# Attention's product with V in two matmuls instead of three: both parts of V as one weight tile, and row differences of V instead of differences of the running products

## The chip, the cores and the metric

The kernel is one launch on one core of a Trainium2 chip. The metric is the device time of an execution in microseconds. Before the change it is 1157.95, the median of three timed executions (1156.58, 1157.95 and 1157.99). Times below are microseconds unless marked otherwise.

## What is computed

The reference is a trunk of two layers on a sequence of 512 tokens of width 1024. Layer 0 mixes the tokens with a stick-breaking attention of 16 heads of 64 columns, layer 1 with a gated token-mixing block; each mixer is followed by a SwiGLU block. All of them stand between RMS norms and a modulation by a conditioning vector. Only the attention bears on this change:

```python
def stick_breaking_attention(q, k, v):
    scale = SB_HEAD_DIM ** -0.5
    for qb in range(S // SB_QBLOCK):
        q0 = qb * SB_QBLOCK
        kend = q0 + SB_QBLOCK
        z = jnp.einsum('bhtd,bhsd->bhts', q[:, :, q0:kend], k[:, :, :kend]) * scale
        before = s_idx < t_idx
        log_beta = jax.nn.log_sigmoid(z)
        log_1m = jnp.where(before, jax.nn.log_sigmoid(-z), 0.0)
        later = lax.cumsum(log_1m, axis=3, reverse=True) - log_1m
        a = jnp.where(before, jnp.exp(log_beta + later), 0.0)
        outs.append(jnp.einsum('bhts,bhsd->bhtd', a, v[:, :, :kend]))
```

A query's weight for an earlier token s is sigmoid(z_s) times the product of sigmoid(-z) over the tokens between s and the query. If r_s is the running product of sigmoid(-z), counted from the query backwards, the weight is the difference of two neighbouring running products. The sum over s of (r before s - r after s) v_s can be regrouped by the running products: each r then multiplies the difference of two neighbouring rows of V.

## The kernel before, in words

The sequence is handed over in reverse order of time, so that "later" runs to the right and one scan along the free dimension forms the running products. Every operand of a matmul is held as two parts, a rounded high part and the rest as a low part, each in a 32-bit matmul type. A product is the sum of three matmuls, high by high, high by low and low by high (`mm3`, L104 to L107). `split` (L112 to L117) makes the two parts: ACT copies the source into the high part, DVE subtracts that from the source.

**Weights** come by DMA from SP's queue into `raw` tiles (two buffers), are split into `wh` (ACT, L159) and `wl` (DVE, L160), and are asked for by `wget` (up to L238) three tiles ahead of use. The columns of the modulation (`G`, `A`, `B` tiles) are summed on DVE out of `rawada` tiles by a background generator; one call of `ada_step` does one step of it.

**The order of instructions.** From the attention stage on PE runs in the order in which the program is written (`pe["chain"]`, set ahead of the second half of V), and DVE from the end of the second half of V until the end of the stage (`dve.chain`). ACT throughout, and DVE ahead of that point, run in the order that the framework's scheduler picks. An engine runs its instructions in that fixed order: one that waits holds up those behind it.

**V.** The projection of V is computed in two halves of 512 columns (8 heads each). `v_step` (L616) adds one of eight contraction steps to four PSUM banks, one for each tile of 128 tokens. `v_evac` (L621) splits the four banks into `Vh` and `Vl` in SBUF (slots at L613 and L614). The first half is done under the start of the layer and evacuated at L739. The second half runs from 64.8 to 90.6 in the trace; between its steps stand the scores of the first pair of heads, and it is evacuated at L933.

**Attention** works on pairs of heads, eight of them, in a loop at the end of the stage (up to L975). Inside a pair (`attend`, L822):

- `scores` (L839) is called for key blocks 3 and 1 together (`B31`), 2 (`B2`) and 0 (`B0`). PE makes z of both heads with three matmuls for each block and head, into two banks `zb`. ACT writes the sigmoid of -z into a tile `ga` (L861). DVE runs one scan along the free dimension, which multiplies the running product by each element (`left`, one tile, shifted by one column), and then subtracts the shifted `left` from `left` back into `ga`: these are the attention weights. There are four `ga` tiles in rotation. Masks `ones` (made with `gaps`) restart the product at the block edges.
- `flip` (L874) turns 128x128 blocks of weights with PE transposes into a bank `tw`, and splits that into `ar` (two buffers): ACT the high part, DVE the low part. It is called for three groups of blocks: `LATE`, `EARLY[0]` and `EARLY[1]`.
- `values` (L888) multiplies with V. For each token block, the V columns of both heads of the pair (128 columns) are the stationary weights, and `ar` of one head is streamed; each of the two heads has its own bank `av` of 128 rows, of which only the 64 rows of that head are used. `mm3` makes it three matmuls.
- `finish` (L903): ACT copies the 64 rows of each head out of `av` into one tile `of` (L909), which is split into `o`, the input of the output projection.

The loop of one pair reads: flip `LATE`, fill, scores `B31` of the next pair, fill, values `LATE`, fill, flip `EARLY[0]`, fill, scores `B2` of the next pair, fill, values `EARLY[0]`, flip `EARLY[1]`, fill, scores `B0` of the next pair, fill, values `EARLY[1]`, finish. A "fill" issues some contraction steps (three matmuls each) of the q and k projections of later pairs (`pqk`; the results are evacuated by `evac_q` and `evac_k`), and once these are done, of the output projection. The number of steps in each gap is written out in `FILLS`, and for pairs 5 to 7 in `LAST`.

In the trace the pairs run from 105.65 (first `tw` of pair 0) to 258.3. In pair 0 the `LATE` values stand at 111.01, those of `EARLY[0]` at 117.94 and those of `EARLY[1]` at 124.72.

Of the kernel before, what the change touches and what calls it, by code (L numbers as in the profile page):

```python
# [13 lines left out]
P = 128  # L14
T = 512
# [16 lines left out]
def trunk(ctx: ExitStack, tc: tile.TileContext, A: dict, out: bass.AP):  # L32
# [16 lines left out]
    def nm(s):  # L49
        uid[0] += 1  # L50
        return f"{s}_{uid[0]}"
# [260 lines left out]
    dve.memset(epsb[:], EPS)  # L312
    oneb = consts.tile([P, 1], F32, name="oneb")
    dve.memset(oneb[:], 1.0)
    sc = consts.tile([P, KD], F32, name="sc")
# [296 lines left out]

    Vh = [[slot(F32R, "Vh") for _ in range(2)] for _ in range(2)]  # L613
    Vl = [[slot(F32R, "Vl") for _ in range(2)] for _ in range(2)]  # L614

# [4 lines left out]

    def v_evac(vb, hf):  # L621
        for tt in range(NT):
            split(Vh[hf][tt // 2][:, tt % 2, :], Vl[hf][tt // 2][:, tt % 2, :], vb[tt][:])

# [113 lines left out]
    fwork["raw"] = ctx.enter_context(tc.tile_pool(name="wraw2", bufs=2))  # L738
    v_evac(vb, 0)  # L739
    o8 = []  # L740
    with tc.tile_pool(name="att", bufs=1) as att, tc.tile_pool(name="att2", bufs=2) as att2:
# [60 lines left out]
        for js in (B31, B2, B0):  # L802
# [12 lines left out]
        left = att.tile([P, 1104], F32, name="left")  # L815
        nc.gpsimd.memset(left[:, :1], 1.0)
        stick = {True: [att.tile([P, 1040], F32, name=nm("ga")) for _ in range(3)],
                 False: [att.tile([P, 528], F32, name=nm("ga"))]}
        for t in stick[True] + stick[False]:
            nc.gpsimd.memset(t[:], 0.0)  # L820

        def attend(i):  # L822
# [5 lines left out]
            weights = {}  # L828
            vc = slice(i % 4 * P, (i % 4 + 1) * P)
            vhf = i // 4  # L830
# [8 lines left out]
            def scores(js):  # L839
# [3 lines left out]
                for j in js:  # L843
                    o, n = offs[j], T - P * j
                    js_ = slice(j * P, (j + 1) * P)
                    for t, (a, b) in enumerate(((0, 0), (0, 1), (1, 0))):
                        for h in range(2):
                            r = slice(64 * h, 64 * h + 64)
                            mm(
                                zb[h][:, o : o + n], q[r, a, js_], kt[r, b, j * P : T],  # L850
                                j == js[0] and t == 0, t == 2,
                            )
                tri, at, M = gaps[js]
                free = stick[js[0] != 2]
                g = free.pop(0)
                free.append(g)
                with tc.issue_after(table.ins):
                    for h in range(2):
                        for j in js:
# [3 lines left out]
                            )  # L863
                dve.tensor_tensor_scan(
                    left[:, 1 : M + 1], g[:, :M], tri, 1.0, ALU.mult, ALU.max
                )
                dve.tensor_tensor(g[:, :M], left[:, :M], left[:, 1 : M + 1], ALU.subtract)
                for h in range(2):
                    for j in js:
                        weights[h, j] = g, at[h, j]  # L870

            turned = {}

            def flip(blocks, h):  # L874

                ps = tw[h]
                n = 0
                for jj, js in blocks:
                    for j in js:
                        g, o = weights[h, j]  # L880
                        o += (jj - j) * P
                        transpose(ps[:, n : n + P], g[:, o : o + P])
                        n += P
                ar = att2.tile([P, 2, T], F32R, tag="ar", name=nm("ar"))
                split(ar[:, 0, :n], ar[:, 1, :n], ps[:, :n])
                turned[blocks[0][0], h] = ar

            def values(blocks, h, stop):  # L888
# [4 lines left out]
                for jj, js in blocks:  # L893
                    w = len(js) * P
                    mm3(
                        av[h][:, js[0] * P : js[0] * P + w],
                        Vh[vhf][jj // 2][:, jj % 2, vc], Vl[vhf][jj // 2][:, jj % 2, vc],
                        ar[:, 0, n : n + w], ar[:, 1, n : n + w],
                        start and n == 0, stop and jj == 3,
                    )  # L900
                    n += w

            def finish():  # L903
# [3 lines left out]
                for h in range(2):  # L907
                    r = slice(64 * h, 64 * h + 64)
                    act.activation(f[r, :], av[h][r, :], AF.Copy)  # L909
                split(o[:, 0, :], o[:, 1, :], f[:])  # L910
# [8 lines left out]
        LATE = ((2, (2,)), (3, (2, 3)))  # L919
        EARLY = ((0, (0,)), (1, (0, 1))), ((2, (0, 1)), (3, (0, 1)))  # L920
        vb = [bank("v1") for _ in range(NT)]
        zb = [bank("z") for _ in range(2)]
        bg0.bank = bg.bank = lambda: zb[0]
        cur = attend(0)
        for k in range(KD):
# [5 lines left out]
            if k > 1:  # L931
                ada_step()
        v_evac(vb, 1)  # L933
        dve.chain = True
# [6 lines left out]
        for i in range(NPAIR):  # L941
# [3 lines left out]
            flip(LATE, 0)  # L945
            flip(LATE, 1)
            fill(next(F))
            if more:
# [14 lines left out]
            flip(EARLY[1], 0)  # L963
            flip(EARLY[1], 1)
            fill(next(F))
            if more:
# [525 lines left out]
```

## Time and profile before

| | before |
|---|---|
| timed executions, median (lowest to highest) | 1157.95 (1156.58 to 1157.99) |
| the profiled execution: time | 1156.4 |
| the profiled execution: span of the trace | 1154.6 |
| granted TensorE clock, mean | 0.996 |
| PE (TensorE matmul) busy | 1133.0, 98% of the span, 7532 instructions |
| PEld (TensorE weight load) busy | 1022.3, 89% |
| DVE (VectorE) busy | 942.3, 82% |
| ACT (ScalarE) busy | 588.1, 51% |
| POOL (GpSimd) busy | 23.9, 2% |
| DMA, mean rate over the span | 151 GB/s |

The span is what the trace covers, from the first to the last instruction; the execution's own time is 1.8 longer. A line of the trace such as `111.01 0.33 PE L93 MATMUL av<-ar,Vh 128*128 128x128 f32 x2` gives the start, the time from the start to the end of the last one, the engine, the line of the kernel, the operation, out and in by the program's names, the shapes and the number of instructions taken together. Line L93 is the helper that issues every matmul, and L69 the one that issues DVE's instructions inside the chain, so that groups are told apart by tiles and shapes and not by lines. A bracket at the end gives how long the engine had stood idle before, and what ended that.

### The profile page before, as it was taken

Reading aid. Unit: us, or ns where it says so; the run is one execution under the profiler, and the core shown is the slowest. Engines: PE = TensorE matmul, PEld = TensorE weight load, DVE = VectorE, ACT = ScalarE, POOL = GpSimd, SP = SyncE. Lnnn points to the kernel's source line nnn. Section 1 sums busy time; section 2 is a strip of 40 time slices with the busy share of each in tenths; the row PEclk is TensorE's granted clock in tenths of the full one; section 3 lists DMA queues with packets and bytes.
Section 4 is the critical chain, followed back from the end, with each engine's and each line's share of the span. In section 5 each row is a group of like instructions: output and inputs, shape, how many; then the busy total and the mean of one; then the engine's idle time right before and its main releaser. Section 6 shows DMA issues by size and latency. Waiting matters only on the chain.

```text
span 1154.6 us, 18784 instructions
## 1 busy us (share of the span) xinstructions
PE 1133.0 (98%) x7532; PEld 1022.3 (89%) x7532; DVE 942.3 (82%) x1214; ACT 588.1 (51%) x977; POOL 23.9 (2%) x43
## 2 busy tenths in 40 slices
PE   6999999999999999999999999999999999999997
PEld 4778888788999999998877898988999999999996
DVE  4988999866998889879686955668979898789996
ACT  6444454645655555554142633526555555565752
POOL 0010000000000000000000100001000000000000
PEclk9999999999999999999999999999999999999999
DMA  8855433114425343338887465324333433223242
GB/s 313 330 183 170 140 111 128 73 56 146 146 92 165 129 148 127 119 118 279 276 283 239 149 231 168 111 70 155 106 125 129 164 129 125 77 91 94 90 163 94
DMA packets 50812, 174.43 MB, mean 151 GB/s; under 512 B 5786, under 2 KB 9114, under 8 KB 50724
## 3 DMA queue, kind: packets, MB, share of 16 engines
q1 hardware_dynamic: 48996, 166.94, 42.7%
q0 software_dynamic: 1728, 6.29, 1.4%
q8 instruction: 59, 0.97, 0.3%
q14 instruction: 29, 0.24, 0.1%
HBM read 164.82 MB, written 8.39 MB: 150 GB/s over the span
## 4 chain that ended last, share of the span: by engine, by line
PE 84%; DMA 6%; DVE 6%; ACT 2%; issue 1%; SPq 0%; DVEq 0%; ACTq 0%
PE r L93 33%; PE y L93 9%; PE v L93 8%; PE pqk L93 7%; PE gu L93 5%; DMA rawada<-in_ada 4%; PE X L93 4%; PE Y L93 3%; PE u L93 3%; PE av L93 3%; PE z L93 2%; PE W L93 1%; PE Z L93 1%; PE tw L101 1%; PE tp L101 1%
## 5 line engine op out<-in xcount | busy, mean ns | idle before, releaser
L93 PE MATMUL r<-Sh,wh 128*128 128x256 f32 x608 | 172.1, 283 | 0.0
L93 PE MATMUL r<-Sl,wh 128*128 128x256 f32 x608 | 172.1, 283 | 0.0
L93 PE MATMUL r<-Sh,wl 128*128 128x256 f32 x608 | 172.1, 283 | 0.0
L93 PE MATMUL y<-wh,as 128*128 128x512 f32 x480 | 150.8, 391 | 0.8 <-DVE G L69 0.8
L159 ACT ACTIVATE wh<-raw 128x1024 fp32r<-128x1024 f32 x87 | 91.6, 1058 | 116.3 <-PE y L93 58.6
L69 DVE TENSOR_TENSOR wl<-f,wh 128x1024 fp32r<-128x1024 f32 x87 | 106.2, 1220 | 39.8 <-ACT wh L116 39.8
L116 ACT ACTIVATE wh<-f 128x1024 fp32r<-128x1024 f32 x87 | 92.2, 1060 | 89.9 <-PE r L93 65.6
L160 DVE TENSOR_TENSOR wl<-raw,wh 128x1024 fp32r<-128x1024 f32 x87 | 105.8, 1219 | 38.5 <-ACT wh L159 34.5
L93 PEld LDWEIGHTS r<-Sh,wh 128*128 128x128 f32 x608 | 116.7, 192 | 0.0
L93 PEld LDWEIGHTS r<-Sl,wh 128*128 128x128 f32 x608 | 116.7, 192 | 0.0
L93 PEld LDWEIGHTS r<-Sh,wl 128*128 128x128 f32 x608 | 116.7, 192 | 0.0
L93 PEld LDWEIGHTS y<-wh,as 128*128 128x128 f32 x480 | 90.1, 188 | 19.7 <-DVE G L69 1.3
L93 PE MATMUL y<-wl,as 128*128 128x512 f32 x240 | 93.7, 390 | 0.0
L93 PE MATMUL r<-hTh,wh 128*128 128x256 f32 x304 | 87.8, 292 | 0.0
L93 PE MATMUL r<-hTl,wh 128*128 128x256 f32 x304 | 85.4, 282 | 0.0
L93 PE MATMUL r<-hTh,wl 128*128 128x256 f32 x304 | 81.0, 283 | 0.0
L93 PE MATMUL r<-hTh,b 128*128 128x256 f32 x304 | 61.0, 283 | 0.0
L93 PEld LDWEIGHTS r<-hTh,wh 128*128 128x128 f32 x304 | 57.9, 191 | 2.4 <-DVE gu L69 0.7
L93 PEld LDWEIGHTS r<-hTl,wh 128*128 128x128 f32 x304 | 58.1, 191 | 0.1
L116 ACT ACTIVATE wh<-rawx 128x1024 fp32r<-128x1024 f32 x38 | 40.3, 1060 | 33.9 <-PE r L93 31.8
L93 PEld LDWEIGHTS r<-hTh,wl 128*128 128x128 f32 x304 | 55.9, 191 | 0.0
L93 PE MATMUL gu<-hTh,wh 128*128 128x256 f32 x192 | 54.6, 285 | 0.0
(266 smaller groups left out, 3026.7 us busy)
## 6 DMA issues: line engine op xcount, KB each, us to landing
rawada<-in_ada SPq DMA_DIRECT2D x80, 512.0 KB, 4.6
rawy<-in_wy SPq DMA_DIRECT2D x38, 512.0 KB, 3.5
rawx<-in_wx SPq DMA_DIRECT2D x38, 512.0 KB, 4.3
raw<-in_wdown SPq DMA_DIRECT2D x22, 512.0 KB, 4.5
raw<-in_wdn SPq DMA_DIRECT2D x22, 512.0 KB, 3.5
raw<-in_wqk SPq DMA_DIRECT2D x16, 512.0 KB, 4.4
ada<-in_ada0p SPq DMA_DIRECT2D x12, 512.0 KB, 8.1
raw<-in_wgu SPq DMA_DIRECT2D x12, 512.0 KB, 3.5
```

The costliest lines, as they stand in the source:

```text
L69: b = getattr(nc.vector, op)(*args, **kw)
L93: b = nc.tensor.matmul(o, l, r, start=start, stop=stop, skip_group_check=True)
L101: last_tp[0] = nc.tensor.transpose(o, i, ident)
L116: act.activation(hi, src, AF.Copy)
L159: act.activation(h[:], raw[:], AF.Copy)
L160: nc.vector.tensor_tensor(l[:], raw[:], h[:].bitcast(F32), ALU.subtract)
```

## The change

**Differences of V.** `Vh` and `Vl` go. For each half and each block of 128 tokens there is a tile `U` of 4 x 256 columns. For each pair of heads it holds the high and low parts of the row differences of V, 64 columns each, in the order high of head 0, low of head 0, low of head 1, high of head 1. The difference of a row is the next row of V minus this row. Since rows lie on partitions, the next row is fetched by DMA: ACT copies V from PSUM to `vf` in SBUF (`v_evac`), POOL issues two DMAs for each block (127 rows shifted by one, and the first row of the next block as the last one; the last block has zeros there), DVE subtracts in place, and the result is split into `U`. There is one buffer `vs` for the shifted copy.

```python
def u_steps(vf, hf, pool):

    def shifted(tt):
        vs = pool.tile([P, 512], F32, tag="vs", name=nm("vs"))
        if tt == NT - 1:
            nc.gpsimd.memset(vs[96:P, :], 0.0)
        nc.gpsimd.dma_start(out=vs[0 : P - 1, :], in_=vf[tt][1:P, :])
        if tt < NT - 1:
            nc.gpsimd.dma_start(out=vs[P - 1 : P, :], in_=vf[tt + 1][0:1, :])
        return vs

    vs = shifted(0)
    yield
    for tt in range(NT):
        dve.tensor_tensor(vs[:], vs[:], vf[tt], ALU.subtract)
        src = vs[:].rearrange("p (a e c) -> p a e c", a=4, e=2)
        dst = U[hf][tt][:].rearrange("p a (q c) -> p a q c", q=4)
        split(dst[:, :, 0::3, :], dst[:, :, 1:3, :], src)
        if tt + 1 < NT:
            vs = shifted(tt + 1)
        yield
```

The first half's steps are all written behind `evac_k` of pair 0, where the scheduler still orders DVE. The second half's stand in the loop of pair 0, inside DVE's fixed order: one step after flip `LATE`, one after values `LATE`, one after each of the two `EARLY` flips. In the built program the four `U` tiles of the second half are called `U_27` to `U_30`.

```diff
+        for _ in u_steps(vf0, 0, att):
+            pass
...
-        v_evac(vb, 1)
+        late_u = u_steps(v_evac(vb), 1, att)
+        next(late_u)
...
             flip(LATE, 1)
+            next(late_u, None)
...
             values(LATE, 1, False)
+            next(late_u, None)
             fill(next(F))
             flip(EARLY[0], 0)
             flip(EARLY[0], 1)
+            next(late_u, None)
...
             flip(EARLY[1], 1)
+            next(late_u, None)
```

**Running products.** The subtraction that made the weights goes; the tile that is turned is now the running product itself. `left` becomes four tiles in rotation and `ga` one tile. The turned block gets one subtracted while it is split: `minus` is a column of -1.

```diff
-                dve.tensor_tensor_scan(
-                    left[:, 1 : M + 1], g[:, :M], tri, 1.0, ALU.mult, ALU.max
-                )
-                dve.tensor_tensor(g[:, :M], left[:, :M], left[:, 1 : M + 1], ALU.subtract)
+                dve.tensor_tensor_scan(r[:, :M], g[:, :M], tri, 1.0, ALU.mult, ALU.max)
...
-                split(ar[:, 0, :n], ar[:, 1, :n], ps[:, :n])
+                act.activation(ar[:, 0, :n], ps[:, :n], AF.Identity, bias=minus)
+                dve.scalar_tensor_tensor(
+                    ar[:, 1, :n], ps[:, :n], 1.0, ar[:, 0, :n].bitcast(F32),
+                    ALU.subtract, ALU.subtract,
+                )
```

**Values.** The 128 stationary columns are now the high and low parts of one head's 64 columns, and all 128 rows of the result are used: 64 hold the product with the high part (the main half), 64 that with the low part (the cross half). Each block takes two matmuls, for the high and the low part of `ar`; low by low is computed as well. `finish` adds the two halves: ACT copies the cross half, DVE adds the main half, once for each head, ahead of the split into `o`.

```diff
-                    mm3(
-                        av[h][:, js[0] * P : js[0] * P + w],
-                        Vh[vhf][jj // 2][:, jj % 2, vc], Vl[vhf][jj // 2][:, jj % 2, vc],
-                        ar[:, 0, n : n + w], ar[:, 1, n : n + w],
-                        start and n == 0, stop and jj == 3,
-                    )
+                    for e in range(2):
+                        mm(
+                            av[h][:, js[0] * P : js[0] * P + w],
+                            U[vhf][jj][:, i % 4, h * P : (h + 1) * P], ar[:, e, n : n + w],
+                            start and n + e == 0, stop and jj == 3 and e == 1,
+                        )
...
-                    act.activation(f[r, :], av[h][r, :], AF.Copy)
+                    main, cross = [slice(64 * e, 64 * e + 64) for e in (h, 1 - h)]
+                    act.activation(f[main, :], av[h][cross, :], AF.Copy)
+                for h in range(2):
+                    main = slice(64 * h, 64 * h + 64)
+                    dve.tensor_tensor(f[main, :], av[h][main, :], f[main, :], ALU.add)
                 split(o[:, 0, :], o[:, 1, :], f[:])
```

More of the change, by code (lines that the diff above doesn't have):

```diff
@@ L611, in trunk @@
     hT = new_hT()
-    Vh = [[slot(F32R, "Vh") for _ in range(2)] for _ in range(2)]
-    Vl = [[slot(F32R, "Vl") for _ in range(2)] for _ in range(2)]
+    U = [[slot(F32R, "U", 4, 256) for _ in range(NT)] for _ in range(2)]
     def v_step(vb, hf, k, w):
@@ L619, in v_step, with v_evac @@
             mm3(vb[tt][:], a, b, w[0][:, k % 2, :], w[1][:, k % 2, :], k == 0, k == KD - 1)
-    def v_evac(vb, hf):
+    def v_evac(vb):
+        vf = [npool.tile([P, 2, 512], F32, tag="n", name=nm("vf")) for _ in range(2)]
+        vf = [vf[tt // 2][:, tt % 2, :] for tt in range(NT)]
         for tt in range(NT):
-            split(Vh[hf][tt // 2][:, tt % 2, :], Vl[hf][tt // 2][:, tt % 2, :], vb[tt][:])
+            act.activation(vf[tt], vb[tt][:], AF.Copy)
+        return vf
+    def u_steps(vf, hf, pool):
[8 more added lines that the diff above has]
+        vs = shifted(0)
+        yield
+        for tt in range(NT):
+            dve.tensor_tensor(vs[:], vs[:], vf[tt], ALU.subtract)
[4 more added lines that the diff above has]
+                vs = shifted(tt + 1)
+            yield
     onec = oneb[:, 0:1]
@@ L814, in trunk @@
             gaps[js] = t, at, n - 1
[L815 to L820, printed above, removed]
+        g = att.tile([P, 1040], F32, name="ga")
+        nc.gpsimd.memset(g[:], 0.0)
+        left = {True: [att.tile([P, 1040], F32, name=nm("left")) for _ in range(3)],
+                False: [att.tile([P, 528], F32, name=nm("left"))]}
         def attend(i):
             weights = {}
-            vc = slice(i % 4 * P, (i % 4 + 1) * P)
             vhf = i // 4
```

25 lines of the change are left out of this document (13 added, 12 removed).

## The prediction

> **What bounds the kernel now.** I read the page first, then the table of stretches, then PE's waits, then the order of time inside one pair of heads.
>
> ```profile
> PE 1133.0 (98%) x7532; PEld 1022.3 (89%) x7532; DVE 942.3 (82%) x1214; ACT 588.1 (51%) x977; POOL 23.9 (2%) x43
> ```
> ```profile
> 105.00:125.60 20.60, 20.60 (x128) 16.74 (x127) 17.00 (x19) 8.79 (x18) 0.00 (x0) 1.00 0.50 157
> 187.20:207.80 20.60, 20.60 (x131) 16.90 (x131) 19.68 (x21) 10.53 (x22) 0.00 (x0) 1.00 0.45 154
> 260.00:290.00 30.00, 29.95 (x140) 24.43 (x139) 20.91 (x31) 16.03 (x34) 1.20 (x2) 1.00 0.39 140
> ```
> ```profile
> PE z L93 <- DVE k L69: 0.9, 1, 0.9
> PE v L93 <- DVE wl L160: 0.8, 1, 0.8
> ```
>
> The first number of a stretch is its length, the second PE's busy time, the fourth DVE's. A pair of heads takes 20.6 us (pair 0 is 105.0 to 125.6), PE is busy all of it, and from 55 to 420 us PE waits for another engine for over half a microsecond only twice. So what leaves PE here shortens the kernel. But DVE is busy 19.68 of 20.60: PE leads by little, and whatever blocks DVE's queue for some microseconds becomes PE's wait.
>
> **What goes.** Each head's product with V loses its third matmul: of 36 a pair, 12 go, 96 in all. Matmuls overlap, so their price is the distance of their starts, not the duration:
>
> ```profile
> 107.78 1.13 PE L93 MATMUL z<-k,q 64*128 64x128 f32 x12
> 108.84 0.50 PE L93 MATMUL pqk<-hTh,wh 128*128 128x512 f32 x1
> ...
> 111.01 0.33 PE L93 MATMUL av<-ar,Vh 128*128 128x128 f32 x2
> 111.18 0.27 PE L93 MATMUL av<-ar,Vl 128*128 128x128 f32 x1
> 111.30 0.45 PE L93 MATMUL av<-ar,Vh 128*128 128x256 f32 x2
> ...
> 112.39 0.40 PE L93 MATMUL pqk<-hTh,wh 128*128 128x512 f32 x1
> ...
> 124.72 0.40 PE L93 MATMUL av<-ar,Vh 128*128 128x256 f32 x2
> ...
> 126.16 0.82 PE L101 MATMUL tw<-identt,ga 128*128 128x128 f32 x6
> ```
>
> Twelve take 112.39 - 111.01 = 1.38 us in the LATE group (the first EARLY group is alike) and 126.16 - 124.72 = 1.44 in the last: 4.2 a pair, 0.117 each. A third of 4.2 is 1.4 a pair, **11.2 us** for eight. Bounds: 0.085 (two of 128 columns in 0.17) gives 8.2; 0.14 (two of 256 in 0.28) gives 13.4. I take the mean.
>
> DVE loses `ga<-left` three times a pair and gains two adds of 64x512:
>
> ```profile
> 110.19 2.30 DVE L69 TENSOR_TENSOR_SCAN left<-ga,ones 128x1027 f32<-128x1027 f32 x1 [2.47 <-ACT ga L861]
> 112.40 1.20 DVE L155 TENSOR_TENSOR wl<-raw,wh 128x1024 fp32r<-128x1024 f32 x1
> 113.52 1.22 DVE L69 TENSOR_TENSOR ga<-left 128x1027 f32<-128x1027 f32 x1
> 114.66 0.69 DVE L69 SCALAR_TENSOR_TENSOR q<-pqk,q 128x512 fp32r<-128x512 f32 x1
> 115.26 1.28 DVE L69 SCALAR_TENSOR_TENSOR A<-rawada,sc,A 128x1024 f32<-128x1024 f32 x1
> 116.45 1.02 DVE L69 TENSOR_TENSOR ar<-tw,ar 128x384 fp32r<-128x384 f32 x2
> 117.38 1.22 DVE L69 TENSOR_TENSOR_SCAN left<-ga,ones 128x513 f32<-128x513 f32 x1
> 118.63 0.69 DVE L69 TENSOR_TENSOR ga<-left 128x513 f32<-128x513 f32 x1
> ```
>
> By starts: scan of 1027 2.2, wl 1.15, stt of 1024 1.2, anything of 512 columns 0.6, a pair of ar of 384 columns 0.95, scan of 513 1.25. The three subtractions are 1.15 + 0.6 + 1.15 = 2.9 a pair, the adds 1.2 (from 0.6, if 64 partitions cost half, to 1.4): DVE gets 1.7 lighter. That earns nothing by itself, since PE ends the stage. The two-instruction split of ar keeps its shapes (Identity with a bias for Copy, stt for a subtraction: q's stt of 512 takes the 0.69 of a subtraction), so no difference. One `ga` for four makes each sigmoid wait for the scan before it; that scan has ended before the next z in every pair.
>
> **What comes.** V now goes to SBUF, is fetched one row shifted by POOL's queue (127 rows of 2 KB, then one row), subtracted and split, four tiles per half, with one buffer `vs`: transfer, subtraction and split of one tile follow each other. Nearest landings, the xd stores of POOL's queue (512 KB) and the raw loads of SP's queue at 50 to 110 us:
>
> ```profile
> DMA to landing us min/median/max: 2.8/3.0/8.1
> ```
> ```profile
> DMA to landing us min/median/max: 3.8/4.5/5.4
> ```
>
> I take 3.0 from first issue to both landed (nearest in queue; half the bytes but two issues); bounds 2.2 and 8.1. The subtraction and split take 0.6 per engine each (512 columns; twice that as upper end). The built order of the changed kernel shows who queues behind. I walk it on before's clock, at three places.
>
> ```profile
> 108.94 1.22 ACT L861 ACTIVATE ga<-z 128x128 f32<-128x128 f32 x4 [1.89 <-PE z L93]
> ...
> 125.64 1.31 ACT L909 ACTIVATE of<-av 64x512 f32<-64x512 f32 x2 [1.89 <-PE av L93]
> 126.97 0.49 ACT L116 ACTIVATE ar<-tw 128x384 fp32r<-128x384 f32 x1
> 127.36 0.63 ACT L116 ACTIVATE o<-of 128x512 fp32r<-128x512 f32 x1
> ```
>
> These are ACT's durations: four sigmoids 1.2, a copy of av 0.65, ar of 384 columns 0.45, 512 columns 0.6.
>
> *Start.*
>
> ```profile
> 67.35 2.59 DVE L69 SCALAR_TENSOR_TENSOR G<-rawada,sc,G 128x1024 f32<-128x1024 f32 x2
> ...
> 70.35 1.13 PE L93 MATMUL z<-k,q 64*128 64x128 f32 x12
> ...
> 72.87 0.50 PE L93 MATMUL v<-wl,hTh 128*128 128x512 f32 x1 [0.77 <-DVE wl L160]
> ```
>
> ACT's four copies of V stand where those of Vh stood, and DVE's four Vl subtractions (0.6 each) go. The first tile's shift lands before DVE asks for it; its subtraction and split take the place of two of those four, so G ends at 70.0 as before, with the first U written at 68.8, and accl follows. The second shift lands at 71.9, its subtraction ends at 72.5. But the new order puts the scan ahead of wl for V's k = 2, and on ACT four sigmoids (1.2) ahead of its wh. z ends at 71.4, sigmoids 72.6, scan 74.9, wl 76.1. PE resumes at 76.15 instead of 72.87: 3.3 lost. The next two shifts end under the 35 matmuls that follow (8 us). Then the G half before `z` of block 0 stands behind a wl whose raw load is later by the same chain: about 0.4. Together **3.7**.
>
> *Pair 0 and 1.* The second half's tiles U_27 to U_30 are not needed before pair 4, yet stand in pair 0's chain on DVE. U_28 ends at 117.2, ar of EARLY[0] behind it: 0.2. The third shift then lands at 120.2, its subtraction ends at 120.8; ACT's half of U_29 at 121.4, DVE's at 122.0, scan 123.25, A 124.45, ar of EARLY[1] 125.05 and 125.65, while PE stands ready at 124.0: 1.05, and PE ends pair 0 at 126.0. The fourth is worse. ACT has its half of U_30 behind both ar of the next flip, and evac_k's Copy behind that; DVE has k, the scan, A, both adds, a wl and o between its half of U_30 and ar. ACT: copies of av until 126.7, ar 127.6, U_30 128.2, k 128.8. DVE: U_30 128.85, k 129.5. `z` of pair 2, which PE reaches at 128.1, waits for k. DVE goes on: scan 131.8, A 133.0, adds 134.25, wl 135.4, o 136.0, ar 136.5 and 136.95. PE's LATE values of pair 1, due 5.35 after the flip's start (flip 0.57, six pqk 1.55, z 1.06, nine pqk 111.01 - 108.84 = 2.17), at 131.35, run at 136.4: 5.05. Together 0.2 + 1.05 + 5.05 = **6.3**. If all U of the second half came before pair 0 or stood aside, this term would be nearly nothing. Pairs 2 to 5 have no U: the adds end 2.9 after the flip's start, o 4.1, ar 4.6 and 5.0, under the 5.35, which hides them by 0.35 at least.
>
> *Pairs 6 and 7.* Fills are shorter. The DVE part of o now waits for ACT's, which waits for both adds, 0.6 more ahead of ar, and PE comes 0.5 to 0.9 earlier. Pair 6 loses 0.3 (the 0.9 of `z` for k goes with `ga<-left`, about the same returns at av), pair 7 1.0: **1.2**. The out projection is reordered a little; PE is busy 29.95 of 30.00 there, and I cost that at nothing.
>
> Sum: -11.2 + 3.7 + 6.3 + 1.2 = **0.0**, on the profiled execution's own 1156.4 (span 1154.6 and 1.8 around it). That run lies at the low end of the timed ones (1156.58 to 1157.99, median 1157.95), so on the median **1158.0**.
>
> [...]
>
> **Rivals.**
>
> *Shifts land late* (slower). SP's loads of the same stretch take 3.8 to 5.4. From 3.6 on, each microsecond costs one at the start (the subtraction passes the sigmoids) and nearly one at U_29, which already waits for its shift. 5.4 gives 1.8 + 2.4 = 4 us, 1162; 8.1 gives about 1171, since U_28 and U_30 join. Against: POOL's median of 3.0.
>
> *One DMA engine moves the 127 rows* (slower).
>
> ```profile
> q0 software_dynamic: 1728, 6.29, 1.4%
> ```
>
> POOL's queue moved 6.29 MB in 1.4% of 16 engines' 1154.6 us, 259 us: 24 KB per us and engine. On one engine 260 KB take 10.7, landing at 12. DVE then stands at each shift: at the start the first lands at 74.6, the second at 89.4, wl ends at 93.5 instead of 72.8, and two later tiles cost 3 each (27 for 3.7); in pairs 0 and 1 each shift comes 5 to 9 us after DVE wants it (28 for 6.3): some 45 more, 1203. No transfer of before has 127 rows. [...]
>
> *A removed matmul is worth more* (faster). At 0.14 each 13.4 go: 1155.8. If PE were held there by its weight loads, each would be worth a whole load:
>
> ```profile
> L93 PEld LDWEIGHTS av<-ar,Vh x192: 186/192/192, 110.8 to 257.7; 128*128 128x128 f32 x192
> ```
>
> 0.19 for each of 96 are 18.2: 1151. Against it stand starts 0.085 to 0.14 apart, less than a load: loads overlap too.
>
> *The change does not take the matmuls out*: excluded, the built program has 96 fewer on PE.
>
> **How the numbers follow.** Forecast, the walk within its own 2.3 us: 0.38, range 1155.7 to 1160.3. Late shifts, or steps of the chain dearer than 0.6: 0.29 (1160.3 to 1166 mostly). One engine: 0.08. Matmul worth more, or tail and chain cheaper (adds at 0.3 each: 0.6 less at pair 1 and at pair 7): 0.25, down to 1150. The range 1150 to 1166 leaves out the single engine and the far ends. 0.2% is 2.3 us, about what a measurement of this kernel can tell from no change: faster 0.25, same 0.38, slower 0.37.
>
> **What would show it.** 24 av matmuls a pair, all from U, starts 0.085 to 0.14 apart, groups of 0.9 to 0.96 us for 1.38 to 1.44. PE's waits: `v` for wl about 4 near 73 us, `av` for ar about 1 near 124, `z` for k and `av` for ar together about 5 near 128 to 137 (3.7 later on after's clock), none in pairs 2 to 5. POOL landings of vs near 3; near 12 the single engine is right. Wrong would be waits of PE in every pair, or none at pair 1: then I misread the order's effect.

## The result, and the profile after

The changed kernel takes **1166.3 us**, the median of six runs (1162.86 to 1167.44), against 1157.26 for the kernel before in its six runs. The ratio is 1.008, with an interval of 1.0064 to 1.0096: slower by 9 us, where no change was forecast and the range ended at 1166. The profiled execution, the slowest of the six, took 1167.44; its span is 1165.7.

The page's first line, instructions and busy time of each engine, in the changed kernel:

```profile
PE 1127.5 (97%) x7436; PEld 1014.1 (87%) x7436; DVE 933.7 (80%) x1215; ACT 596.0 (51%) x985; POOL 30.0 (3%) x55
```

PE has its 96 matmuls less, and DVE is 8.6 us less busy. Neither made the kernel faster, so the time went into waits. PE's waits from 55 to 420 us (total, times, longest), which before were two of 0.8 and 0.9 us and a few shorter ones:

```profile
PE av L93 <- DVE ar L69: 6.0, 5, 2.8
PE v L93 <- ACT wh L159: 5.4, 1, 5.4
PE v L93 <- DVE wl L160: 2.7, 1, 2.7
PE z L93 <- DVE G L69: 1.0, 1, 1.0
PE z L93 <- ACT k L116: 0.7, 1, 0.7
PE av L93 <- DVE of L69: 0.7, 1, 0.7
PE z L93 <- ACT ga L884: 0.5, 1, 0.5
PE z L93 <- DVE k L69: 0.5, 1, 0.5
```

By stretches, with the granted clock as the first of the three numbers after the engines' times, pair 0, pair 1 and a pair in the middle read:

```profile
117.10:138.80 21.70, 19.72 (x118) 15.37 (x116) 15.31 (x20) 10.83 (x21) 4.08 (x7) 1.00 0.40 120
138.80:165.00 26.20, 21.45 (x118) 16.66 (x117) 21.42 (x24) 12.28 (x25) 0.00 (x0) 0.93 0.38 123
184.20:203.40 19.20, 19.20 (x119) 15.46 (x118) 17.86 (x20) 10.97 (x22) 0.00 (x0) 1.00 0.44 136
```

The middle pair is what was hoped for: PE busy throughout, 19.2 us for 20.6. Pair 0 has holes, pair 1 has holes and a lower clock. For all kernels below, three stretches of the trace are set side by side: **start**, from the first matmul of V's second half (where PE waited ahead of it, from when it stood ready) to the first `tw` of pair 0; **pairs**, from there to the end of pair 7; **rest**, from there to the end of the span.

| profiled execution | start | pairs 0 and 1 | pairs, all eight | rest |
|---|---|---|---|---|
| before | 40.8 | 20.5, 20.5 | 152.4 | 896.5 |
| changed | 51.3 | 21.7, 26.2 | 152.8 | 895.7 |

So 10.4 us were lost at the start, and in the pairs the matmuls' gain was lost again. The stretch ahead of the start differs by 1.1 us between the two profiled executions (64.8 and 65.9) and the rest by 0.8 the other way. In the thirteen kernels of this study the stretch ahead varies from 62.5 to 65.9 and the rest from 894.6 to 897.7; those differences are not the change's.

**The start.** DVE of the changed kernel, and POOL's first shift:

```profile
66.76 0.69 DVE L69 TENSOR_TENSOR k<-pk,k 128x512 fp32r<-128x512 f32 x1
71.52 0.69 DVE L69 TENSOR_TENSOR vs<-vs,vf 128x512 f32<-128x512 f32 x1 [4.08 <-DMA vs<-vf]
...
77.40 0.69 DVE L69 TENSOR_TENSOR vs<-vs,vf 128x512 f32<-128x512 f32 x1 [0.81 <-DMA vs<-vf]
78.01 2.29 DVE L69 TENSOR_TENSOR_SCAN left<-ga,ones 128x1027 f32<-128x1027 f32 x1
80.22 1.20 DVE L160 TENSOR_TENSOR wl<-raw,wh 128x1024 fp32r<-128x1024 f32 x1
```
```profile
63.64 0.67 POOL L635 DMA_DIRECT2D vs<-vf  x1 [2.35 <-ACT vf L626]
64.30 0.51 POOL L637 DMA_DIRECT2D vs<-vf  x1
```

DVE stands still for 4.08 us at the first shift, with two G sums and `accl` behind it, and `wl`, which PE needs, comes at 80.22 instead of 71.59. ACT stands behind DVE, and `wh`, which PE needs first, comes only after that:

```profile
72.30 0.63 ACT L116 ACTIVATE U<-vs 128x512 fp32r<-128x512 f32 x1 [5.58 <-DVE vs L69]
75.24 0.63 ACT L116 ACTIVATE acch<-G 128x512 fp32r<-128x512 f32 x1 [2.31 <-DVE G L69]
75.78 1.19 ACT L884 ACTIVATE ga<-z 128x128 f32<-128x128 f32 x4
76.83 1.08 ACT L159 ACTIVATE wh<-raw 128x1024 fp32r<-128x1024 f32 x1
```

The landing of the shifts, first of those issued from 60 to 70 us, then of those from 70 to 80:

```profile
DMA to landing us min/median/max: 7.1/7.3/7.5
```
```profile
DMA to landing us min/median/max: 2.5/2.6/2.8
```

The first was issued within 1 us of four loads of 512 KB on SP's queue (two of `raw`, two of `rawada`, issued from 62.6 to 64.4) and landed after 7.1 and 7.5; the busy share of the DMA engines was 0.83 to 1.10 in each microsecond from 65 to 71, and 0.06 in the next. The second, issued after two microseconds with a share of 0.00, took 2.5 and 2.8; the median of all is 3.1.

PE in the same stretch:

```profile
71.46 1.13 PE L93 MATMUL z<-k,q 64*128 64x128 f32 x12
77.96 0.79 PE L93 MATMUL v<-wh,hTh 128*128 128x512 f32 x1 [5.37 <-ACT wh L159]
81.47 0.79 PE L93 MATMUL v<-wl,hTh 128*128 128x512 f32 x1 [2.71 <-DVE wl L160]
82.06 0.63 PE L93 MATMUL v<-wh,hTl 128*128 128x512 f32 x1
82.49 0.63 PE L93 MATMUL v<-wh,hTh 128*128 128x512 f32 x1
...
85.47 0.40 PE L93 MATMUL v<-wl,hTh 128*128 128x512 f32 x1
85.71 0.40 PE L93 MATMUL v<-wh,hTl 128*128 128x512 f32 x1
```

The waits are 8.1 us where there was 0.8. And when PE resumes, its matmuls start 0.43 us apart instead of 0.23, until 85.3: about 2 us more. The granted clock is 0.50 from 75.2 to 85.4.

**Pair 1** ends the same way:

```profile
146.66 0.33 PE L93 MATMUL av<-ar,U 128*128 128x128 f32 x1 [0.68 <-DVE of L69]
149.81 1.45 PE L93 MATMUL av<-ar,U 128*128 128x128 f32 x7 [2.83 <-DVE ar L69]
151.06 0.63 PE L93 MATMUL pqk<-hTh,wh 128*128 128x512 f32 x1
151.49 0.63 PE L93 MATMUL pqk<-hTl,wh 128*128 128x512 f32 x1
...
154.25 0.48 PE L93 MATMUL pqk<-hTh,wh 128*128 128x512 f32 x1
154.57 0.40 PE L93 MATMUL pqk<-hTl,wh 128*128 128x512 f32 x1
```

Its four waits (0.74 and 0.51 of `z` for `k`, 0.68 and 2.83 of `av`) make 4.76 us; the matmuls after them run at half rate for three microseconds (granted clock 0.50 from 150.3 to 153.7).

### The profile page after: what moved, and what is told of

Its sections match the earlier page's. It is cut to its first block, busy times and chain, and to the rows that moved or that the text cites. A ratio compares the mean times of both kernels' runs of the same rounds, so it can differ in the third digit from the quotient of the medians.

```text
span 1165.7 us, 18660 instructions
## 1 busy us (share of the span) xinstructions
PE 1127.5 (97%) x7436; PEld 1014.1 (87%) x7436; DVE 933.7 (80%) x1215; ACT 596.0 (51%) x985; POOL 30.0 (3%) x55
## 4 chain that ended last, share of the span: by engine, by line
PE 71%; DVE 8%; DMA 5%; ACT 2%; issue 1%; DVEq 0%; SPq 0%; ACTq 0%
PE r L93 32%; PE y L93 8%; PE pqk L93 4%; DMA rawada<-in_ada 4%; PE X L93 4%; PE v L93 4%; PE gu L93 4%; PE Y L93 3%; PE u L93 3%; PE av L93 2%; DVE wl L160 1%; PE W L93 1%; PE Z L93 1%; DVE t L69 1%; PE z L93 1%
## 5 line engine op out<-in xcount | busy, mean ns | idle before, releaser
L93 PEld LDWEIGHTS y<-wh,as 128*128 128x128 f32 x480 | 90.0, 188 | 19.4 <-DVE G L69 0.9
L93 PE MATMUL r<-hTl,wh 128*128 128x256 f32 x304 | 85.4, 282 | 0.0
L93 PE MATMUL v<-wh,hTh 128*128 128x512 f32 x128 | 52.2, 408 | 7.1 <-ACT wh L159 5.4
```

The costliest lines, as they stand in the source:

```text
L93: b = nc.tensor.matmul(o, l, r, start=start, stop=stop, skip_group_check=True)
```

## The experiments

Theory A: an engine whose queue is in fixed order (DVE, then whichever engine takes its place) stands at a shift that has not landed, and PE runs slowly after each long wait. Theory B: the added steps cost this much wherever they stand and whoever does them.

### The matmuls alone (e4_two)

```diff
-                    mm3(
-                        av[h][:, js[0] * P : js[0] * P + w],
-                        Vh[vhf][jj // 2][:, jj % 2, vc], Vl[vhf][jj // 2][:, jj % 2, vc],
-                        ar[:, 0, n : n + w], ar[:, 1, n : n + w],
...
+                    for e in range(2):
+                        mm(
+                            av[h][:, js[0] * P : js[0] * P + w],
+                            Vh[vhf][jj // 2][:, jj % 2, vc], ar[:, e, n : n + w],
```

> The kernel before without its third matmul with V (high part of ar by low part of V is left out, so the result lacks that term); nothing else is changed, DVE's work included. By the prediction's price, 0.117 us a matmul, 11.2 us go: 1146. Rival: DVE, busy 19.68 of a pair's 20.60 us, becomes the bound once PE needs 19.2, so that a pair of heads gains 0.9 us at most: 7 us, 1150. If a removed matmul were worth its weight load, 18 us: 1139.

The kernel leaves out the product of the high part of `ar` with the low part of V.

Measured: 1147.07, ratio 0.9922 (0.9899 to 0.9945) to a kernel before of 1155.45. Start 40.9; pairs 0 and 1 19.14 each, 1.37 less, which is 0.114 for a matmul; all pairs 143.5, 9.0 less. Pairs 2 to 4 stay at 19.4, since DVE is as busy as before (940.5 us in all, 942.3 before). The price was right (0.117 forecast); DVE as the bound took back 0.2 in each of these pairs, not 0.5 (and 0.8 in pair 5, with 18.7 where e13_defer below has 17.9).

### The second half's steps spread (e2_spread)

```diff
-        vf = [npool.tile([P, 2, 512], F32, tag="n", name=nm("vf")) for _ in range(2)]
+        vf = [
+            npool.tile([P, 2, 512], F32, tag="n", name=nm("vf")) if not own
+            else slot(F32, "vf")
+            for _ in range(2)
+        ]
...
             flip(LATE, 1)
             next(late_u, None)
...
             values(LATE, 1, False)
-            next(late_u, None)
...
             flip(EARLY[0], 1)
-            next(late_u, None)
...
             flip(EARLY[1], 1)
-            next(late_u, None)
```

> The second half's four U steps stand one in each of pairs 0 to 3, behind flip LATE, and vf of that half has slots of its own; everything else as in the change. Theory A (the steps stall DVE because each waits for its own shift and they crowd into one pair): pairs 0 and 1, which took 21.7 and 26.2 us, come back to 19.2 to 19.5 like pairs 2 to 5, with no wait of PE over half a microsecond: 9 us less, 1157. The prediction's walk had 6.3 us there: 1160. Theory B (a step costs DVE 1.4 us plus a hop to ACT, and DVE has no room for it in any pair): pairs 0 to 3 take over 20.5 us each, and at most 3 us are gained, 1163 or more.

Measured: 1160.11, ratio 1.0032 (1.0017 to 1.0047). Start 51.4, unchanged. Pairs 0 to 3 took 19.2, 20.4, 20.9 and 20.4, where the change had 21.7, 26.2, 19.2 and 19.2: 8.4 gained in the first two, 2.9 given back in the next two. So the crowding into pair 0 was the greater part, as A has it, and B holds for the rest: in pairs 1 to 3, where the adds and `o` stand ahead of `ar`, DVE has no room for a step. PE's waits from 55 to 420 us say where:

```profile
PE av L93 <- DVE ar L69: 4.6, 5, 1.3
```

### The first half's steps behind the scan (e3_first)

```diff
-        for _ in u_steps(vf0, 0, att):
-            pass
+        u0 = u_steps(vf0, 0, att)
+        next(u0)
...
                 cur[0](B31 if k == 1 else B2)
+            if 1 <= k <= 4:
+                with tc.issue_after(scan[0].ins):
+                    next(u0)
```

> The first half's U steps are queued on DVE behind the scan of block B31 of pair 0; everything else as in the change. Theory A (DVE stood still for the first shift, which landed 7.5 us after its issue, and PE then ran at half clock): the scan still stands ahead of wl, so PE still waits about 3 us near 73 us, but not 8.1, and no stretch at half clock follows; the end of V's second half comes about 6 us earlier, 1160. Theory B (the added copies, subtractions and splits cost this much by themselves, whenever they stand): V's second half ends within 2 us of the changed kernel's, 1164 to 1166.

Measured: 1170.06, ratio 1.0128 (1.0102 to 1.0154), slower than the change. At its place the edit did most of what A said: V's waits fell from 5.4 and 2.7 to 2.4 and 1.8, and V's second half ended 25.6 us after the scores of B31 began (29.6 in the change, 20.2 before). But PE then waited 7.1 us for G ahead of block 0, and the start was 55.7. Ahead of G, DVE stood 3.45 us at the shift of the first half's last tile; and the load of `g`, by which G is multiplied, left SP only at 97.3, 0.8 into PE's wait. The next run bears on the second.

### Both, and the old order at the start (e6_pin)

To the two edits above it adds that the sigmoids and the scan of B31 of pair 0 stand behind `wh` and `wl` of the second weight tile of V's second half:

```diff
-                with tc.issue_after(table.ins):
+                hi, low = parts["wv", 1, 1] if i == 0 and js is B31 else (table, None)
+                with tc.issue_after(hi.ins):
...
-                dve.tensor_tensor_scan(r[:, :M], g[:, :M], tri, 1.0, ALU.mult, ALU.max)
+                with tc.issue_after(low.ins) if low else ExitStack():
+                    scan[0] = dve.tensor_tensor_scan(r[:, :M], g[:, :M], tri, 1.0, ALU.mult, ALU.max)
```

> The change with both edits (first half's U steps behind the scan, second half's one in each of pairs 0 to 3), and with the sigmoids and the scan of B31 of pair 0 queued behind wh and wl of the next V weights, the order of the kernel before. Theory A: nothing of the start's loss of 9.3 us is left but about 0.5, nothing of the 9.7 us of pairs 0 and 1 but about 1, and the matmuls' 11 us stay: 1148. Theory B: the steps cost the same at their new places, 1160 or more.

Measured: 1165.14, ratio 1.0071 (1.0046 to 1.0096). V's second half ended 19.1 us after the scores began, with no wait at all: every microsecond that the change had lost there is gone, so shift and order together were its cause, and the added steps themselves cost nothing at this place (against B). The pairs took 147.4, as in the run that only spread the steps. But the start was 56.2. PE's wait, SP's queue, and DVE at the end of it:

```profile
PE z L93 <- DVE G L69: 14.0, 1, 14.0
```
```profile
72.35 21.36 SPq L110 DMA_DIRECT2D raw<-in_wqk  x7
93.76 0.42 SPq L110 DMA_DIRECT2D g<-in_post_g  x1
```
```profile
100.28 0.69 DVE L69 TENSOR_TENSOR G<-z,g 128x512 f32<-128x512 f32 x1 [4.93 <-DMA g<-in_post_g]
```

The load of `g` stands on SP behind seven weight loads, each of which waits for a `raw` buffer. In the kernel before it was issued at 62.4, behind two weight loads; in the change at 91.3, behind three `wqk` loads, late but not last. The forecast never looked at SP's queue here: the reordering of it came with the change.

### g loaded first (e7_g)

To e6_pin it adds that `g` of the G sum is allocated and loaded (`row`) ahead of G's own loads, and not where it is used:

```diff
+            if len(self.parts) == 1:
+                row(*self.parts[0][2:])
             for name, at, s, part in self.parts:
```

> The kernel with the second half's steps spread, the first half's behind the scan and the old order of wh and wl at the start, and in addition the load of g (the gain that G's second sum is multiplied by) issued first of G's loads and not after the weight loads. Theory A': the 14.0 us for which z of block 0 waited for G were SP's queue, in which g stood behind seven weight loads that waited for their buffers; with g loaded ahead they go, 1152, and what is left above 1146 is the room that DVE lacks in pairs 1 to 3 (4.3 us) and about 1 at the start. Rival: DVE itself is late with G, and the wait stays above 8 us: 1160 or more.

Measured: 1161.88, ratio 1.0057 (1.0035 to 1.008). The wait of `z` fell from 14.0 to 1.4, so SP's queue was its main cause. But V's first matmuls of the second half now waited 5.5 us for `wh`, until 71.1. This was not a load: the `raw` tiles had left SP at 49.3 and 54.3 and landed by 59.6. In ACT's order `acch` of the G sum now stood ahead of this `wh`, and waited for the last two sums of G on DVE:

```profile
69.47 0.63 ACT L116 ACTIVATE acch<-G 128x512 fp32r<-128x512 f32 x1 [3.07 <-DVE G L69]
70.01 1.99 ACT L160 ACTIVATE wh<-raw 128x1024 fp32r<-128x1024 f32 x2
```

In the change the first `wh` of that half was made at 57.7 and `acch` at 75.2. Start 51.5. The wait had moved once more, from SP's queue to ACT's.

### POOL in place of DVE (e8_pool)

```diff
-            dve.tensor_tensor(vs[:], vs[:], vf[tt], ALU.subtract)
+            nc.gpsimd.tensor_tensor(vs[:], vs[:], vf[tt], ALU.subtract)
...
-            split(dst[:, :, 0::3, :], dst[:, :, 1:3, :], src)
+            hi, low = dst[:, :, 0::3, :], dst[:, :, 1:3, :]
+            act.activation(hi, src, AF.Copy)
+            nc.gpsimd.tensor_tensor(low, src, hi.bitcast(F32), ALU.subtract)
```

> The change with one edit: the subtraction of the shifted rows and the low part of U are done by POOL instead of DVE, at the same places of the program. Theory A (DVE's queue stands still at each shift): PE's waits for DVE in pairs 0 and 1 (ar, k) fall from 5.7 us to about 1, and at the start only the scan ahead of wl is left, 3 us: 1154 at best. Theory B (the chain of transfer, subtraction and split is itself too slow, and ACT, which does the high parts, stands at it just as DVE did): PE's waits move from DVE to ACT, and the time stays above 1162.

Measured: 1162.93, ratio 1.0068 (1.0043 to 1.0094). PE's waits for `ar` fell to 2.1 us in all, but pair 1 took 27.0: `z` waited 3.7 for a sigmoid, on ACT behind a high part of U. The start fell to 48.5. ACT had taken DVE's place at the shift, as B said for ACT, though the mechanism is A's: a fixed queue and a transfer that has not landed.

### POOL, spread, g first (e9_pool)

The edits of e8_pool, e2_spread and e7_g together.

> U's subtractions and low parts on POOL, the second half's steps one in each of pairs 0 to 3, and the load of g issued first of G's loads; the rest as in the change. Theory A: nothing is left on DVE that waits for a shift, no wait of PE over 1.5 us at the start and none in the pairs, the matmuls' gain stays: 1147. Theory B: as in the run before, ACT stands at the steps, 1155 or more.

Measured: 1163.49, ratio 1.007 (1.0051 to 1.0088). The pairs took 143.1 in all, 19.1 to 19.2 for each of the first five: nothing of the pairs' loss is left, and DVE's lack of room is settled. The start was 57.5. V waited 5.5 for `wh` as in e7_g, and PE another 5.2 for q, since ACT stood 7.7 us at the first half's last U tile with the evacuation of V's banks behind it:

```profile
105.48 0.63 ACT L660 ACTIVATE U<-vs 128x512 fp32r<-128x512 f32 x1 [7.68 <-POOL vs L656]
106.02 2.04 ACT L639 ACTIVATE vf<-v 128x512 f32<-128x512 f32 x4
```

In both kernels with `g` first the first shift is not issued among the four loads; here it landed after 3.0 to 3.3 us (3.0 to 3.4 in e7_g).

### PE kept busy through the wait (e10_warm)

```diff
+            if k == 1:
+                wb = bank("warm", "p")
+                for n in range(26):
+                    mm(wb[:], hTk(hT, n % 4, 0, P)[0], wv[0][:, 1, :], n == 0, n == 25)
```

> The change with 26 matmuls of 512 columns more, into a bank that nothing reads, right behind the scores of B31 of pair 0, where PE stood still for 8 us. If the slow matmuls after the wait (0.43 us from start to start in place of 0.23) come from PE having stood still, they go, and V's second half ends about 1.6 us earlier after its wl: 1164.5. If they come from something else at that place (weights or hT not ready, DMA traffic), the spacing stays at 0.43 and the time at 1166.

Measured: 1171.47, ratio 1.0146 (1.0125 to 1.0168). PE's order of time:

```profile
70.39 6.19 PE L93 MATMUL warm<-wh,hTh 128*128 128x512 f32 x26
76.42 0.39 PE L93 MATMUL v<-wh,hTh 128*128 128x512 f32 x1
79.51 0.51 PE L93 MATMUL v<-wl,hTh 128*128 128x512 f32 x1 [2.70 <-DVE wl L160]
...
80.56 0.55 PE L93 MATMUL v<-wh,hTl 128*128 128x512 f32 x1
80.90 0.63 PE L93 MATMUL v<-wh,hTh 128*128 128x512 f32 x1
...
83.89 0.48 PE L93 MATMUL v<-wl,hTh 128*128 128x512 f32 x1
84.20 0.39 PE L93 MATMUL v<-wh,hTl 128*128 128x512 f32 x1
```

The 26 matmuls filled the first wait, and the one right behind them ran at full rate (0.39 us, where the change's first took 0.79). The second wait, 2.70 us, was enough by itself: four matmuls at 0.23 to 0.24 apart, then half rate from 80.6 to 84.0, where the granted clock is 0.50. So the question came out halfway. The slow stretch came with PE standing still (2.70 us) and not with the weights at that place (the first matmul after the fill was fast on the same weight tile), but it does not take 8 us of it, and it was not removed. The added matmuls also moved the order of the steps behind them (PE waited 2.6 us more for V's evacuation), which makes the time of this run unfit for a price.

### POOL and spread, the shift released early (e11_pools)

To the edits of e8_pool and e2_spread it adds:

```diff
-            nc.gpsimd.tensor_tensor(vs[:], vs[:], vf[tt], ALU.subtract)
-            src = vs[:].rearrange("p (a e c) -> p a e c", a=4, e=2)
+            nc.gpsimd.tensor_tensor(vf[tt], vs[:], vf[tt], ALU.subtract)
+            if tt + 1 < NT:
+                vs = shifted(tt + 1)
+            src = vf[tt].rearrange("p (a e c) -> p a e c", a=4, e=2)
```

> U's subtractions and low parts on POOL, the second half's steps one in each of pairs 0 to 3, the difference written over vf so that the next shift leaves right after the subtraction; g's load and the start's order as the scheduler sets them. Theory A: the pairs take 19.1 to 19.2 us each as with the run before on POOL, with no wait of PE in them (9.7 us less than the change). At the start ACT stands at the first U for the late shift, with the sigmoids and wh behind it, as in the run that had only POOL in place of DVE: 5 us lost there. Together 1152. Theory B (the time at the start is not the first shift's but that of all four steps): 3 us less at the start too, as the steps overlap now: 1149.

Measured: 1153.45, ratio 0.9981 (0.9966 to 0.9996), below the kernel before. Pairs 143.1; start 50.5, with 3.5 us of waiting for `wh` and 3.5 for `wl`: the overlap of the four steps did not help there. The first shift took 8.1 us to land, with ACT at its U tile and `wh` behind it, and the scan still stood ahead of `wl`.

### The same, with the start pinned (e12_pin)

ACT and DVE at the start as in e6_pin, the first two U tiles' high parts behind V's last `wh`, the other two behind the sigmoids of B2, and the weight loads written after `g` held behind it:

```diff
+        with tc.issue_after(ahead[0].ins) if len(ahead) == 1 else ExitStack():
+            load(raw[:], src)
...
+            if k in (1, 4):
+                with tc.issue_after(parts["wv", 1, 3][0].ins if k == 1 else last_act[0].ins):
+                    next(u0)
+                    next(u0)
```

> The same, and at the start wh and wl of the next V weights queued ahead of the sigmoids and the scan, U's high parts behind wh and the sigmoids on ACT, g's load ahead of the weight loads that come later in the program. Theory A: nothing stands at a shift any more, neither at the start (under 1 us lost) nor in the pairs, and the matmuls' 11 us are all there: 1146 to 1148, below the kernel before. Theory B: some other queue takes the wait over once more (g's load on SP as in the runs with the pinned start, or PE's v at a weight load), and the time is 1152 or more.

Measured: 1153.47, ratio 0.9972 (0.9955 to 0.9989). V waited 1.0 us, pairs 143.1, start 48.6: `z` of block 0 waited 4.35 us for ACT, and half rate followed. ACT's order of time at that place:

```profile
91.05 0.63 ACT L657 ACTIVATE U<-vf 128x512 fp32r<-128x512 f32 x1 [6.49 <-POOL vf L651]
91.58 1.04 ACT L157 ACTIVATE wh<-raw 128x1024 fp32r<-128x1024 f32 x1
92.53 0.61 ACT L116 ACTIVATE acch<-G 128x512 fp32r<-128x512 f32 x1
```

### The last two U tiles out of the way (e13_defer)

```diff
         cur[0](B0)
+        with tc.issue_after(last_act[0].ins):
+            for tt in rest:
+                u_split(vf0, 0, tt)
```

`rest` holds tiles 2 and 3 of the first half, and `u_split` is the split of one tile.

> The run before (U on POOL, second half spread, start pinned, g ahead) with one edit: the high parts of the first half's last two U tiles are queued on ACT behind the sigmoids of block 0 instead of among the weight splits. Theory A (each wait left is ACT standing at a U tile whose shift has not been subtracted yet): the 4.35 us for which z of block 0 waited, and the stretch at half clock after it (2 us), go: 1147. Theory B (PE waits there for the weight loads themselves): the wait moves to the next weight tile, 1153.

Measured: **1148.89**, ratio 0.9933 (0.9909 to 0.9957). PE's longest waits from 55 to 420 us:

```profile
PE z L93 <- DVE G L69: 3.0, 1, 3.0
PE av L93 <- DVE ar L69: 1.2, 2, 0.7
PE z L93 <- DVE accl L69: 0.6, 1, 0.6
```

ACT's wait is gone, as A said; pairs 143.1, start 45.5. Of the 10.4 us that the change lost at the start 4.6 are left: 3.0 of `z` for G, which stands on DVE behind a `wl` whose `raw` load left SP late, 0.6 for `accl`, and a stretch at half rate behind the 3.0, less 1.1 by which V's second half ended sooner after the scores than before. This version beats the kernel before by 7 us and the change by 17.

## Why the prediction was wrong, step by step

**Matmuls, -11.2: right.** In the pairs with nothing in the way (all of e13_defer) each of pairs 0 to 4 is 1.34 to 1.42 us shorter, against 1.4. All eight pairs gain 9.3; the forecast had 10.0 (11.2 less 1.2 for pairs 6 and 7, which gained 0.7 and 0.1 in the change, 1.1 and 0.4 forecast). That DVE's lighter load earns nothing by itself is nearly right: e4_two, without it, loses 0.2 in each of pairs 2 to 4 and 0.8 in pair 5.

**Start, +3.7: wrong, +10.4 measured.** This is the step that failed, by 6.7; the term of pairs 0 and 1 below was short by 3.4. (In the profiled spans 10.4 at the start, 0.3 in all eight pairs and 0.3 outside make the 11.0 between 1154.6 and 1165.7; the medians differ by 9.0.) Its input was a landing of 3.0 us for every shift, from POOL's transfers elsewhere in the trace. That is the median that came out (3.1), but the one shift that DVE stands at first took 7.5. The rival of late shifts had the rule ("from 3.6 on, each microsecond costs one at the start") and with 7.5 gives 3.9 more, so 7.6: most of the wait. The walk had PE wait for `wl` behind the scan, 3.3; the trace has 2.7 for that, and 5.4 ahead of it for `wh`, on ACT, which stood at the first U tile. The late landing goes with the traffic in the eleven kernels with the shift: in the nine in which the four loads left SP within a microsecond of it the first shift took 6.5 to 8.1, in the two in which they did not (e7_g, e9_pool) 3.0 to 3.4. (No run moves these four loads and nothing else, so that they are its cause is the author's reading.) The walk took a median where the traffic of that microsecond was in the trace of before: three loads of 512 KB leave SP there from 61.5 to 62.8.

**Half rate: missing.** No step had it. In the change it cost about 2 us at the start and 1.7 in pair 1 (six matmuls 0.2 later each, the rest in `av`). The traces show the rate (0.43 from start to start for 0.23), the length (3.4 us, from 80.6 to 84.0 in e10_warm), and that 2.70 us of waiting were enough (e10_warm). From 55 to 420 us of the thirteen traces, each of PE's waits of 2.70 us or more has matmuls at half rate behind it, from at most 1.7 us after its end (e13_defer, 97.1 and 98.8), and no wait of 1.43 or less (e7_g, at 99.4) brought any. Between these the length does not decide: 1.66 was followed by it (e3_first, wait at 140.0; the six `tw` next in line took 1.48, in the change 0.82), 1.74 (the change, at 136.1) and 2.56 (e10_warm, at 100.0) were not. As an estimate, with 1.6 (eight matmuls 0.2 later each) to 2 us (as measured at the start) more behind each of the walk's two long waits (3.3 and 5.05) the forecast would have been 1161 to 1162, with the late shift 1165 to 1166.

**Pairs 0 and 1, +6.3: right in mechanism, 9.7 measured** (against the undisturbed 19.16 and 19.10 of e13_defer). The waits were named one by one: 5.05 in pair 1 for `z` and `av` is 4.76 in the trace, in the same order; pair 0's 1.25 is 2.0. Of the other 2.9, 1.7 is half rate; what is left was not taken apart. "If all U of the second half came before pair 0 or stood aside, this term would be nearly nothing" holds with POOL (e9_pool), not with DVE (e2_spread): the walk had not counted that a step also needs DVE's time in a pair.

**One `ga` tile, at nothing: half right.** In pairs 0 to 5 of e13_defer, which have no delay, no PE wait follows from it; in pair 1 of the change ACT's sigmoids waited 3.15 us for the scan before.

**z for G, +0.4: 1.0 in the change.** The walk's reason is what the trace shows: G at 103.86 stands on DVE behind a `wl`, whose `wh` had waited 2.02 us for its `raw` load. What it missed is that `g` itself had left SP 29 us later than before. With the start pinned (e6_pin) that load decides, and the wait is 14.0 us.

**The rivals.** One DMA engine for 127 rows is out: it was priced at 10.7 us, and the second shift's 127 rows landed in 2.8 with the DMA engines idle (share 0.00 ahead of it). That one engine might take them was the author's assumption, which no run shows. A matmul worth its whole weight load (0.19) is out by e4_two (0.114). Late shifts, at 0.29, was the case that came, but in full only for the first shift (7.5; the 127 rows of the others took 2.8 to 5.4), where the rival's higher price had nearly all of them late. Its price had no half rate in it, and so the range ended at 1166.

What stays open: why the framework's scheduler issues `g` so late in the changed kernel (91.3, and 87.8 to 97.3 in the six other kernels in which its load was not moved); no run isolates what makes it so. Open too is what decides, for a wait between 1.4 and 2.7 us, whether half rate follows.

## What to carry to other kernels

A transfer that an engine in fixed order waits for has to be priced by what the other queues have in flight at the moment it is issued, not by the median of its kind (here 7.5 us, with a median of 3.1), and the step that waits belongs on an engine that nobody waits for. When a wait is removed, look through every queue that was reordered by the same edit, the DMA-issuing one too, for the next wait in line: here it moved from DVE to SP and to ACT, and the gain showed only with all of them out of the way. And a wait of TensorE of 2.7 us or more cost, in each of the eleven traces here that have one, its length and a stretch at half rate behind it (matmuls 0.43 us apart for 0.23).

## What was not expected of the hardware

- The two transfers of a shift on POOL's queue took 2.8 us (254 KB) and 2.3 us (2 KB) from issue to landing at their quickest in the change, 4.4 to 5.4 beside weight loads, and 6.5 to 8.1 when four loads of 512 KB left SP within a microsecond of it. In the change the 2 KB of the first shift took 7.1, the two `raw` loads issued 1.2 to 1.7 us ahead of them 4.0 and 5.1: the small transfer did not come out ahead of the loads.
- Behind a wait of 2.70 us PE ran at half rate for 3.4 us, beginning one microsecond after it had resumed (e10_warm); behind the waits of 0.68 and 2.83 us in pair 1, with one matmul between them, it began 0.5 us after. In the change the granted clock is 0.50 for 3.4 us there (150.3 to 153.7), and for 10.2, three times that, at the start (75.2 to 85.4).
- POOL took 1.28 us for a subtraction of 128x512 out of SBUF (e12_pin, at 70.18), DVE 0.69 (the change, at 71.52); POOL's ran up to 2.28 (e13_defer) and a `wl` of DVE up to 2.35 (1.23 alone; e12_pin) where the two overlap, though not in every overlap. Even so POOL carried all of U's subtractions without a wait of PE over 0.73 us in the pairs (e9_pool, e11_pools, e12_pin, e13_defer).
- An add of 64 partitions x 512 on DVE took 0.66 to 0.70, as long as a subtraction of 128 (0.69).
